# Attention in a decoder trunk: the two heads that share a 128-feature block are handled together, their matmuls side by side in halves of the array

## The chip, the cores and the metric

The kernel runs on one core of a Trainium2 chip. The metric is the device time of one execution in microseconds (us); the median of three runs before the change is 1267.95 us (1264.78 to 1268.28). The engines are named as the profile names them: PE (TensorE matmuls), PEld (its weight loads), DVE (VectorE), ACT (ScalarE), POOL (GpSimd) and SP (which here only issues DMAs).

## The reference

One inference step of a two-layer decoder trunk for a prompt of 512 tokens and 8 single-token samples (520 columns in all), model width 1024, all in float32. What matters here are two attentions; the rest (projections, retention in layer A, squared-ReLU MLPs of width 4096, norms) is untouched.

```
def memory_attention(q, mk, mv):                      # 4 heads of 64, 256 memory tokens, in both layers
    s = einsum('blhd,bmhd->bhlm', q, mk) * MEM_HD ** -0.5
    p = softmax(s, axis=-1)
    return einsum('bhlm,bmhd->blhd', p, mv)

def windowed_sink_attention(q, k, v, qpos, kpos, sinks):   # layer B: 12 heads of 64 over 4 kv heads
    dist = qpos[:, :, None] - kpos[:, None, :]
    valid = (kpos >= 0) & (dist >= 0) & (dist <= WINDOW)
    s = einsum('bnqgrd,bnkgd->bngrqk', q, k) * hd ** -0.5
    s = s - slopes * dist
    s = where(valid, s, -inf)
    p = sink_softmax(s, sink)                         # max over keys and the head's sink; the sink is in the sum
    return einsum('bngrqk,bnkgd->bnqgrd', p, v)
```

## The kernel before, in words

Activations lie feature-major: 128 features on the partitions, 520 tokens along the free axis. The big products (projections and MLP) use a split of every float32 operand into a high and a low part in a faster format (`product`, L233; three matmuls for each pair of tiles). The attentions use plain float32 matmuls; each of these appears in the trace as two PE records ("passes"), each with its own weight load.

Two heads of 64 features lie in one 128-feature block: head half `hh` = 0 on partitions 0 to 63, `hh` = 1 on partitions 64 to 127. A score matmul contracts over 64 features, so it uses 64 rows of the array (64\*128 in the trace); a value matmul ("PV" from here) gives 64 output features, so it uses 64 columns (128\*64).

**`mem_attention`** (L492 on; tiles `ms`, `p`, `mt`, `mpT`, `mo`) loops over the block `bl` (2) and the half `hh` (2). For each half it makes the scores of 4 blocks of 128 queries against 256 memory tokens, two blocks in one PSUM bank (L502), a softmax (row maximum on DVE L504, exp on ACT L506, scaling on DVE L511), transposes the probabilities on PE (L516), copies them out of PSUM (L518) and multiplies by the values, 512 columns at a time (L519). It runs in both layers.

**`win_pair`** (L653 on; tiles `ws`, `wp`, `wt`, `wpT`, `wo`) is called once for each of two blocks of kv heads `kb`, as the generators `w` and `W`, and loops over 4 query blocks `qb` and the halves `hh`. One half has three query heads: three score matmuls over 256 keys (128 in the first query block) into two PSUM banks of the role `ws` (L666), three additions of the distance penalty that read those banks (DVE L671), the sink softmax (L675 to L684 on DVE, exps on ACT L681), the scaling (L686, two of the three on POOL), three transposes for each key block (L692), a copy (ACT L694) and the PV matmul over 384 columns (L695). After both halves the output is split into its high and low part for the output projection (`Pair.put`, L177 on ACT and L178 on DVE).

PSUM has eight banks, given to roles: `mm` three (accumulators of the projections), `ws` two, `wt` two, `ot` one.

What sets the order: each phase is written as generators whose steps are woven by a string (`ORDER_A` for layer A with the memory attention as `a`; `ORDER_B` for layer B with `k` and `q` the projections, `a` the memory attention, `w`/`W` the two window generators, `s`/`S` the samples, `o` output projections). A step ends at `yield`. A scheduler then places the instructions of each engine, taking the string as the priority; where an instruction isn't ready it puts later matmuls ("filler": projection matmuls, L233) ahead of it.

Of the kernel before, what the change touches and what calls it, by code (L numbers as in the profile page):

```python
# [3 lines left out]

# [45 lines left out]
BUFS_A = dict(blk=2, qkv=6, wp=2, wpT=2, qw=1, kvs=1, ld=5)  # L50
BANKS = dict(mm=3, ws=2, wt=2, ot=1)
ORDER_A = "mhhhmhhhshkkhshkhshshkkkakhaakghhaghhhggghg"
ROLE_W = "ws"
BUFS_B = dict(blk=2, wp=4, wpT=6, ld=5)
# [5 lines left out]
ORDER_B = "kasakkskasqqsaqwqwqwqWWooSSSoSowWoWoo"  # L60
# [55 lines left out]
def build(tc, d, o):  # L116
    nc = tc.nc
    with ExitStack() as ctx:
# [372 lines left out]

        def mem_attention(l, qm, out):  # L492
            kT, v = memkv[l]
            for bl in range(2):
                for hh in range(2):
                    r = slice(64 * hh, 64 * hh + 64)
                    p = [blk(f"p{l}{bl}{hh}{qp}", [P, 2, MEM], "wp") for qp in range(2)]
                    for qp in range(2):
                        s = ps(f"ms{l}{bl}{hh}{qp}", "ws").rearrange("p (b m) -> p b m", b=2)
                        for b in range(2):  # L500
                            q0 = (2 * qp + b) * P
                            nc.tensor.matmul(s[:, b, :], qm[bl][r, q0:q0 + P], kT[r, bl, :], start=True, stop=True)  # L502
                        nm, sm, ri = (small(n, [P, 2]) for n in ("nm", "sm", "ri"))
                        nc.vector.tensor_reduce(out=nm, in_=s, axis=AX.X, op=ALU.max, negate=True)  # L504
                        for b in range(2):
                            nc.scalar.activation(out=p[qp][:, b, :], in_=s[:, b, :], func=AF.Exp,  # L506
                                                 bias=nm[:, b:b + 1], accum_out=sm[:, b:b + 1])
                        nc.vector.reciprocal(out=ri, in_=sm)
                        for b in range(2):
                            pb = p[qp][:, b, :]  # L510
                            nc.vector.tensor_scalar(out=pb, in0=pb, scalar1=ri[:, b:b + 1], scalar2=None, op0=ALU.mult)  # L511
                    pv = ps(f"mo{l}{bl}{hh}", "ot")
                    for mh in range(2):
                        t = ps(f"mt{l}{bl}{hh}{mh}", "wt")
                        for qb in range(NCH):
                            nc.tensor.transpose(t[:, qb * P:qb * P + P], p[qb // 2][:, qb % 2, mh * P:mh * P + P], ident)  # L516
                        pT = blk(f"mpT{l}{bl}{hh}{mh}", [P, T], "wpT")
                        (nc.scalar.copy if mh else nc.vector.tensor_copy)(out=pT, in_=t)  # L518
                        nc.tensor.matmul(pv[r, :], v[:, mh, (2 * bl + hh) * 64:(2 * bl + hh) * 64 + 64], pT,  # L519
                                         start=mh == 0, stop=mh == 1)  # L520
                    out.put(6 + bl, pv[r, :], slice(0, T), r)
                    yield
# [130 lines left out]
        def win_pair(kb, q, kT, vt, out, role):  # L653
            for qb in range(NCH):
                qs = slice(qb * P, qb * P + P)
                k0 = 0 if qb else P
                nk = 2 * P - k0
                ks = slice((qb - 1) * P + k0, qb * P + P)
                ot = ps(f"wo{kb}{qb}", "ot")
                for hh in range(2):  # L660
                    r = slice(64 * hh, 64 * hh + 64)
                    g = 2 * kb + hh
                    s = [ps(f"ws{g}{qb}{i}", role if i else "ws").rearrange("p (b m) -> p b m", b=2) for i in range(2)]
                    sv = [s[i // 2][:, i % 2, k0:] for i in range(3)]
                    for i in range(3):
# [410 lines left out]
```

## Time and profile before

| what | value |
|---|---|
| median of the three runs | 1267.95 us |
| the profiled execution's own time | 1268.36 us |
| its span, first to last instruction | 1266.0 us |
| PE busy | 1225.8 us (97%) |
| DVE busy | 861.7 us (68%) |
| ACT busy | 541.0 us (43%) |
| POOL busy | 309.5 us (24%) |
| mean granted TensorE clock | 0.979 of full speed |

The median and the profiled execution differ by 0.4 us, and the latter spends 2.4 us outside its span. A busy share is a mean over phases: layer A lies at about 0 to 288 us, its MLP follows, layer B with the window attention lies at about 688 to 863 us, and the second MLP ends the program. PE's busy time counts the tail of each matmul's pipeline, so for what a group of matmuls costs, the start of the next group in the timeline is the better reading.

### The profile page before, as it was taken

The page shows a single profiled execution, that of the slowest core. Times are in us where ns is not written, and L with a number is a line of the kernel's source. Part 1 is how long each engine was busy: PE and PEld are TensorE (multiplying, and loading weights), DVE is VectorE, ACT ScalarE, POOL GpSimd, SP SyncE. Part 2 cuts the span into 40 slices and gives each one's busy share as a digit, 9 for nine tenths or more (in the row PEclk, how much of TensorE's full clock was granted, in tenths as well). Part 3 has the DMA queues.
Part 4 walks back from the last instruction along what each step waited for, and adds up shares of the span by engine and source line. Part 5 has one row for each costly group of instructions (what it writes and reads, how often), then busy time and mean ns, then how long its engine had stood idle before and what let it go on. Part 6 is the DMA issues. An engine that isn't in the chain of part 4 may idle for free. (4 is left out here: it accounts for less than half of the span.)

```text
span 1266.0 us, 23737 instructions
## 1 busy us (share of the span) xinstructions
PE 1225.8 (97%) x9670; PEld 1152.8 (91%) x9670; DVE 861.7 (68%) x1615; ACT 541.0 (43%) x1019; POOL 309.5 (24%) x271
## 2 busy tenths in 40 slices
PE   8999999998899999999999999999799999999996
PEld 7999978898899999999999777577689999999996
DVE  7676766779886667666457556577996666676733
ACT  6232432234564444444324335445464444444532
POOL 2201100029321212121024112316731212131112
PEclk9999999998899999999999999899799999999998
DMA  8245512120232223232324341301123222222412
GB/s 303 103 152 181 196 58 82 69 101 34 84 113 88 101 85 117 84 117 84 117 84 141 132 147 45 123 1 35 34 101 111 90 101 100 92 95 98 143 41 69
DMA packets 43789, 128.26 MB, mean 101 GB/s; under 512 B 5112, under 2 KB 10368, under 8 KB 43552
## 3 DMA queue, kind: packets, MB, share of 16 engines
q1 hardware_dynamic: 41440, 119.80, 27.6%
q0 software_dynamic: 2240, 6.95, 1.5%
q8 instruction: 76, 1.25, 0.4%
q14 instruction: 33, 0.27, 0.1%
HBM read 117.65 MB, written 9.08 MB: 100 GB/s over the span
## 5 line engine op out<-in xcount | busy, mean ns | idle before, releaser
L433 DVE TENSOR_TENSOR xs<-d,xs 128x264 f32<-128x264 f32 (+1 forms) x128 | 53.9, 422 | 105.1 <-PE d L233 105.1
L785 ACT ACTIVATE u<-u 128x520 f32<-128x520 f32 x64 | 40.8, 637 | 29.6 <-DVE u L784 29.6
L233 PE MATMUL d<-hid,dw 128*128 128x256 f32 (+1 forms) x384 | 46.9, 283 | 0.0
L233 PEld LDWEIGHTS d<-hid,dw 128*128 128x128 f32 x384 | 46.3, 188 | 0.1
L619 POOL DMA_DIRECT2D out_ret_s<-s x12 | 6.8, 569 | 130.0 <-DVE S L599 64.7
L686 POOL TENSOR_SCALAR wp<-wp,wsm 128x256 f32<-128x256 f32 (+1 forms) x32 | 16.8, 535 | 68.8 <-DVE wsm L684 28.4
L784 DVE SCALAR_TENSOR_TENSOR u<-u,f0r 128x520 f32<-128x520 f32 x32 | 28.7, 898 | 0.4
L784 DVE SCALAR_TENSOR_TENSOR u<-u,f1r 128x520 f32<-128x520 f32 x32 | 28.6, 897 | 0.4
L681 ACT ACTIVATE wp<-wp,wnm 128x256 f32<-128x256 f32 (+1 forms) x48 | 22.7, 474 | 11.4 <-DVE wes L678 5.9
L233 PE MATMUL ob<-obh,obw 128*128 128x256 f32 (+1 forms) x128 | 26.0, 290 | 0.4 <-ACT obh L177 0.4
L178 DVE TENSOR_TENSOR hid<-u,hid 128x520 fp32r<-128x520 f32 x32 | 24.4, 761 | 0.0
L666 PE MATMUL ws<-kvb,qb 64*128 64x256 f32 (+1 forms) x96 | 23.9, 381 | 0.0
L233 PEld LDWEIGHTS ob<-obh,obw 128*128 128x128 f32 x128 | 20.4, 188 | 2.8 <-ACT obh L177 1.3
L671 DVE SCALAR_TENSOR_TENSOR wp<-cb,ws 128x256 f32<-128x256 f32 (+1 forms) x48 | 16.0, 380 | 6.8 <-PE ws L666 6.6
L177 ACT CAST hid<-u 128x520 fp32r<-128x520 f32 x32 | 20.1, 627 | 1.0
L253 POOL TENSOR_TENSOR f<-f0t,f 128x260 fp32r<-128x260 f32 x12 | 11.8, 982 | 33.6 <-ACT f L252 33.6
L666 PEld LDWEIGHTS ws<-kvb,qb 64*128 64x128 f32 x96 | 16.0, 192 | 4.3 <-issue 0.5
L695 PE MATMUL wo<-wpT,kvb 128*64 128x384 f32 x56 | 19.1, 530 | 0.7 <-ACT wpT L694 0.3
L694 ACT COPY wpT<-wt 128x384 f32<-128x384 f32 x28 | 12.6, 478 | 15.7 <-PE wt L692 15.5
L233 PE MATMUL ob<-obl,obw 128*128 128x256 f32 (+1 forms) x64 | 17.7, 292 | 0.3 <-DVE obl L178 0.3
L252 ACT CAST f<-f0t 128x260 fp32r<-128x260 f32 x16 | 6.5, 407 | 26.7 <-DVE f0t L263 26.7
L416 DVE SCALAR_TENSOR_TENSOR qb<-qb,br 128x256 f32<-128x256 f32 (+1 forms) x12 | 5.1, 425 | 18.2 <-PE qb L233 18.1
(2056 smaller groups left out, 5253.0 us busy)
## 6 DMA issues: line engine op xcount, KB each, us to landing
kc<-in_mem_k SPq DMA_DIRECT2D x16, 256.0 KB, 3.7
vc<-in_mem_v SPq DMA_DIRECT2D x16, 256.0 KB, 3.8
s<-in_S SPq DMA_DIRECT2D x12, 256.0 KB, 5.5
out_ret_s<-s POOLq DMA_DIRECT2D x12, 256.0 KB, 2.6
xs<-in_xT SPq DMA_DIRECT2D x8, 260.0 KB, 4.3
memx<-in_memT SPq DMA_DIRECT2D x1, 1024.0 KB, 8.6
u000r<-in_w_up SPq DMA_DIRECT2D x2, 512.0 KB, 3.1
u002r<-in_w_up SPq DMA_DIRECT2D x2, 512.0 KB, 3.9
```

The costliest lines, as they stand in the source:

```text
L177: nc.scalar.copy(out=self.hi(kt, sl, rows), in_=src)
L178: eng.tensor_sub(out=self.lo(kt, sl, rows), in0=src, in1=f(self.hi(kt, sl, rows)))
L233: nc.tensor.matmul(t, w[:, ws], a(kt, HALVES[s]), start=kt == k[0] and m == 0, stop=kt == k[-1] and m == 2)
L433: nc.vector.tensor_add(out=x[mb][:, ts], in0=t, in1=x[mb][:, ts])
L666: nc.tensor.matmul(sv[i], q[3 * kb + i][r, qs], kT[r, ks], start=True, stop=True)
L671: nc.vector.scalar_tensor_tensor(out=pv[:, i, :], in0=cb["nd"][:, k0:], scalar=float(SLOPES[hq + i]), in1=sv[i], op0=ALU.mult, op1=ALU.add)
L681: nc.scalar.activation(out=pv[:, i, :], in_=pv[:, i, :], func=AF.Exp, bias=nm[:, i:i + 1], accum_out=sm[:, i:i + 1])
L686: (nc.gpsimd if i in POOL_N else nc.vector).tensor_scalar(out=pv[:, i, :], in0=pv[:, i, :], scalar1=sm[:, i:i + 1], scalar2=1.0, op0=ALU.m ...
L694: nc.scalar.copy(out=pT, in_=t[:, 0:3 * P])
L695: nc.tensor.matmul(ot[r, 0:3 * P], vt[:, qb - 1 + kk, g * 64:g * 64 + 64], pT, start=kk == k0 // P, stop=kk == 1)
L784: nc.vector.scalar_tensor_tensor(out=u[i], in0=u[i], scalar=0.0, in1=r[0], op0=ALU.max, op1=ALU.mult)
L785: nc.scalar.square(out=u[i], in_=u[i])
```

## The change

`side_by_side` is new: it takes pairs of matmuls and adds an order-only dependency from each matmul to the one before it, so that the scheduler keeps the sequence half 1, half 0, half 1, half 0. `mem_attention` and `win_pair` handle both halves in one step: the scores of both (rows 0 to 63 and 64 to 127 of the array, into different PSUM banks), then, after a `yield`, the transposes of both and their PV matmuls (columns 0 to 63 and 64 to 127, into one bank). A window block's softmax now runs over six heads at once (`[P, 6]` statistics), its four score banks are two of `ws` and two of `mm` (`ROLE_W`), and the memory attention's output is split once for 128 partitions instead of twice for 64. Buffers change with it (`BUFS_A`, `BUFS_B`), and `ORDER_B` gives each window block two letters, one for the scores and one for the rest. In the changed file the lines move: scores and PV of both attentions are issued at L499, the transposes at L532 and L709, the window's additions at L686, its reduction at L690, its exps at L696 and its scaling at L701.

```
-BUFS_A = dict(blk=2, qkv=6, wp=2, wpT=2, qw=1, kvs=1, ld=5)
+BUFS_A = dict(blk=2, qkv=6, wp=2, mp=4, wpT=3, qw=1, kvs=1, ld=5)
-ROLE_W = "ws"
-BUFS_B = dict(blk=2, wp=4, wpT=6, ld=5)
+ROLE_W = "mm"
+BUFS_B = dict(blk=2, wp=3, mp=4, wpT=6, ld=5)
-ORDER_B = "kasakkskasqqsaqwqwqwqWWooSSSoSowWoWoo"
+ORDER_B = "kasakkskasqqsaqwqwqwwqWwWWwWooSSSoSowWWowoWWoo"
...
+        def side_by_side(*pairs):
+            last = None
+            for pair in pairs:
+                for m in reversed(pair):
+                    i = m()
+                    if last is not None:
+                        tc.add_manual_dep(i.ins, last.ins.name, mybir.DependencyInfo(
+                            mybir.DependencyClass.NoSync, mybir.DependencyReason.DATA), reason="side by side")
+                    last = i
...
             for bl in range(2):
-                for hh in range(2):
-                    r = slice(64 * hh, 64 * hh + 64)
-                    p = [blk(f"p{l}{bl}{hh}{qp}", [P, 2, MEM], "wp") for qp in range(2)]
-                    for qp in range(2):
-                        s = ps(f"ms{l}{bl}{hh}{qp}", "ws").rearrange("p (b m) -> p b m", b=2)
...
+                for qp in range(2):
+                    s = [ps(f"ms{l}{bl}{hh}{qp}", "ws").rearrange("p (b m) -> p b m", b=2) for hh in range(2)]
+                    side_by_side(*([partial(nc.tensor.matmul, s[hh][:, b, :], qm[bl][r, (2 * qp + b) * P:(2 * qp + b + 1) * P], kT[r, bl, :],
+                                            start=True, stop=True) for hh, r in enumerate(rows)] for b in range(2)))
...
+                yield
+                pv = ps(f"mo{l}{bl}", "ot")
+                for mh in range(2):
...
+                    side_by_side([partial(nc.tensor.matmul, pv[r, :], v[:, mh, (2 * bl + hh) * 64:(2 * bl + hh) * 64 + 64], pT[hh],
+                                          start=mh == 0, stop=mh == 1) for hh, r in enumerate(rows)])
-                    out.put(6 + bl, pv[r, :], slice(0, T), r)
+                out.put(6 + bl, pv, slice(0, T))
...
         def win_pair(kb, q, kT, vt, out, role):
...
+                s = [[ps(f"ws{kb}{qb}{hh}{i}", role if i else "ws").rearrange("p (b m) -> p b m", b=2) for i in range(2)]
+                     for hh in range(2)]
+                side_by_side(*([partial(nc.tensor.matmul, sv[hh][i], q[3 * kb + i][r, qs], kT[r, ks], start=True, stop=True)
+                                for hh, r in enumerate(rows)] for i in range(3)))
+                p = blk(f"wp{kb}{qb}", [P, 6, 2 * P], "wp")
...
+                m, nm, sm, es = (small(f"w{i}", [P, 6]) for i in ("m", "nm", "sm", "es"))
...
+                yield
...
+                    side_by_side([partial(nc.tensor.matmul, ot[r, 0:3 * P], vt[:, qb - 1 + kk, (2 * kb + hh) * 64:(2 * kb + hh) * 64 + 64],
+                                          pT[hh], start=kk == k0 // P, stop=kk == 1) for hh, r in enumerate(rows)])
```

How the instructions move, at three places. First PE near the end of layer B, before the change: the scores of one half (`ws320`: kv head 3, query block 2, bank 0), the PV matmuls of another (`wo03`: kb 0, query block 3; `wpT03` is kv head 0, the first half) and the first transpose (`wt13`) of the second half of that block.

```order
L666 MATMUL ws320_9741<-kvb_7825,qb0_7823 128x256
L666 MATMUL ws320_9741<-kvb_7825,qb1_7824 128x256
L666 MATMUL ws321_9742<-kvb_7825,qb1_7824 128x256
L695 MATMUL wo03_9613<-wpT030_9644,kvb_7825 64x384
L695 MATMUL wo03_9613<-wpT031_9651,kvb_7825 64x384
L692 MATMUL wt130_9680<-c_77,wp13_9659 128x128
```

The change, PE, in the middle of the window blocks: the six scores of block kb 1, qb 1 (the third digit of `ws1110` is the half), then the four PV matmuls of block kb 0, qb 1.

```order
L499 MATMUL ws1110_9129<-kvb_7819,qb0_7817 128x256
L499 MATMUL ws1100_9127<-kvb_7819,qb0_7817 128x256
L499 MATMUL ws1110_9129<-kvb_7819,qb1_7818 128x256
L499 MATMUL ws1100_9127<-kvb_7819,qb1_7818 128x256
L499 MATMUL ws1111_9130<-kvb_7819,qb1_7818 128x256
L499 MATMUL ws1101_9128<-kvb_7819,qb1_7818 128x256
L499 MATMUL wo01_8890<-wpT0110_8941,kvb_7819 64x384
L499 MATMUL wo01_8890<-wpT0100_8935,kvb_7819 64x384
L499 MATMUL wo01_8890<-wpT0111_8955,kvb_7819 64x384
L499 MATMUL wo01_8890<-wpT0101_8949,kvb_7819 64x384
```

The halves, which stood in separate groups, now alternate.

Second, PE in the memory attention of layer A after the change (`ms`: layer, block, half, query pair; `rt` is a transpose of the retention, `ga` a gate projection).

```order
L499 MATMUL ms0111_2122<-memk0_1089,orq1_97 128x256
L595 MATMUL rt40_2398<-c_77,k4_2000 128x128 x3
L499 MATMUL ms0101_2121<-memk0_1089,orq1_97 128x256
L499 MATMUL ms0111_2122<-memk0_1089,orq1_97 128x256
L499 MATMUL ms0101_2121<-memk0_1089,orq1_97 128x256
L595 MATMUL rt40_2398<-c_77,k4_2000 128x128
L234 MATMUL ga101_2589<-ah1_189,ga1h_2558 128x264
L499 MATMUL mo00_2060<-mpT0011_2089,memv0_1090 64x512
L499 MATMUL mo00_2060<-mpT0001_2082,memv0_1090 64x512
```

Here the first matmul of the sequence stands alone, ahead of other work, and three follow together; the two PV matmuls stand together.

Third, PE at the end of layer B's window blocks after the change: the end of block kb 0, qb 3, then matmuls of the samples (`wst`, `wso`, `wsx`), then the scores of kb 1, qb 2.

```order
L499 MATMUL ws0311_9545<-kvb_7819,qb0_7817 128x256
L499 MATMUL ws0301_9543<-kvb_7819,qb0_7817 128x256
L756 MATMUL wst1_9461<-c_77,wsp1_9416 128x128
L757 MATMUL wst1_9461<-c_77,wsp1_9416 8x128
L763 MATMUL wso1_9468<-wvn_9312,wpn_9466 128x256
L770 MATMUL wso1_9468<-vwc4_9470,wspT1_9464 32x256 x2
L770 MATMUL wso1_9468<-vwc6_9475,wspT1_9464 32x256 x2
L776 MATMUL wsx1_9482<-c_77,wsosb1_9480 128x128 x2
L499 MATMUL ws1210_9585<-kvb_7819,qb0_7817 128x256
```

Before the change these sample matmuls stood among output-projection matmuls; here none stands between them.

## Rows read from the trace of the kernel before

**Rows 1.** The page, busy time, share and instructions of each engine (first line).

```profile
PE 1225.8 (97%) x9670; PEld 1152.8 (91%) x9670; DVE 861.7 (68%) x1615; ACT 541.0 (43%) x1019; POOL 309.5 (24%) x271
```

**Rows 2.** Windows of the attention stretches: us, busy PE, PEld, DVE, ACT, POOL, granted clock, DMA.

```profile
150.00:230.00 80.00, 80.00 (x572) 66.92 (x571) 53.15 (x146) 27.32 (x61) 4.84 (x8) 1.00 0.22 78
690.00:748.00 58.00, 58.00 (x397) 44.33 (x397) 31.91 (x81) 19.72 (x54) 9.81 (x7) 1.00 0.37 117
748.00:785.30 37.30, 37.30 (x228) 28.54 (x227) 24.05 (x85) 17.61 (x61) 10.44 (x17) 1.00 0.20 61
785.30:815.40 30.10, 28.06 (x157) 17.46 (x156) 19.60 (x66) 17.07 (x55) 12.85 (x15) 0.83 0.52 173
815.40:863.00 47.60, 46.43 (x297) 35.08 (x297) 29.19 (x123) 21.40 (x84) 7.51 (x15) 1.00 0.00 1
```

**Rows 3.** Groups by line (forms apart or mixed): count, busy us, mean ns, idle before.

```profile
L666 PE MATMUL ws<-kvb,qb 64*128 64x256 f32 (+1 forms) x96 | 23.9, 381 | 0.0
L502 PE MATMUL ms<-memk,orq 64*128 64x256 f32 x32 | 9.5, 408 | 0.0
L502 PE MATMUL ms<-memk,qb 64*128 64x256 f32 x32 | 8.2, 392 | 0.0
L519 PE MATMUL mo<-mpT,memv 128*64 128x512 f32 x32 | 16.1, 610 | 0.0
L695 PE MATMUL wo<-wpT,kvb 128*64 128x384 f32 x56 | 19.1, 530 | 0.7 <-ACT wpT L694 0.3 <-DVE obl L178 0.3
L233 PE MATMUL d<-hid,dw 128*128 128x256 f32 (+1 forms) x384 | 46.9, 283 | 0.0
```

**Rows 4.** Timeline of PE around two score groups: start us, us, operation, count.

```profile
172.23 1.13 PE L502 MATMUL ms<-memk,orq 64*128 64x256 f32 x4
173.29 0.39 PE L233 MATMUL qkv<-ah,qkv42l 128*128 128x256 f32 x1
...
759.41 0.28 PE L233 MATMUL qb<-bh,qb4h 128*128 128x256 f32 x1
759.62 1.56 PE L666 MATMUL ws<-kvb,qb 64*128 64x256 f32 x6
761.11 0.38 PE L233 MATMUL qb<-bl,qb4h 128*128 128x256 f32 x1
```

**Rows 5.** Timeline of PE around three PV groups of the window attention.

```profile
766.53 0.86 PE L695 MATMUL wo<-wpT,kvb 128*64 128x384 f32 x2
767.32 0.39 PE L233 MATMUL qb<-bh,qb4l 128*128 128x264 f32 x1
...
852.99 1.50 PE L695 MATMUL wo<-wpT,kvb 128*64 128x384 f32 x4
854.42 0.39 PE L233 MATMUL ob<-obl,obw 128*128 128x264 f32 x1
...
794.71 1.52 PE L695 MATMUL wo<-wpT,kvb 128*64 128x384 f32 x8
796.16 0.39 PE L233 MATMUL ob<-obl,obw 128*128 128x256 f32 x1
```

**Rows 6.** Timeline of PE at the longest idle gap of the window attention.

```profile
800.60 0.68 PE L723 MATMUL wss<-kwc,qdw 128*32 128x129 f32 x8 [1.64 <-DVE wp L671]
```

**Rows 7.** Groups by line with forms apart: the window softmax between scores and transposes.

```profile
L671 DVE SCALAR_TENSOR_TENSOR wp<-cb,ws 128x256 f32<-128x256 f32 x36 | 13.2, 413 | 5.9 <-PE ws L666 5.8
L675 DVE TENSOR_REDUCE wm<-wp 128x3 f32<-128x768 f32 x12 | 11.4, 948 | 0.1
L681 ACT ACTIVATE wp<-wp,wnm 128x256 f32<-128x256 f32 x36 | 18.0, 500 | 8.9 <-DVE wes L678 4.7 <-DVE wnm L677 4.0
L681 ACT ACTIVATION_READ_ACCUMULATOR wp<-wp,wnm 128x1 f32 x48 | 9.1, 189 | 0.0
L686 POOL TENSOR_SCALAR wp<-wp,wsm 128x256 f32<-128x256 f32 x24 | 12.8, 545 | 54.0 <-DVE wm L676 28.1 <-DVE wsm L684 20.1 <-DVE wes L678 3.7
L694 ACT COPY wpT<-wt 128x384 f32<-128x384 f32 x28 | 12.6, 478 | 15.7 <-PE wt L692 15.5
```

More of the change, by code (lines that the diff above doesn't have):

```diff
@@ L3 @@
 from contextlib import ExitStack, contextmanager
+from functools import partial
 import numpy as np
@@ L494, in mem_attention @@
             for bl in range(2):
-                for hh in range(2):
-                    r = slice(64 * hh, 64 * hh + 64)
-                    p = [blk(f"p{l}{bl}{hh}{qp}", [P, 2, MEM], "wp") for qp in range(2)]
-                    for qp in range(2):
-                        s = ps(f"ms{l}{bl}{hh}{qp}", "ws").rearrange("p (b m) -> p b m", b=2)
-                        for b in range(2):
[L501 to L506, printed above, removed]
+                p = {}
@@ L653, in win_pair @@
         def win_pair(kb, q, kT, vt, out, role):
+            rows = [slice(0, 64), slice(64, P)]
             for qb in range(NCH):
@@ L656, in win_pair @@
                 k0 = 0 if qb else P
[L657 removed]
                 ks = slice((qb - 1) * P + k0, qb * P + P)
+                kbs = range(k0 // P, 2)
                 ot = ps(f"wo{kb}{qb}", "ot")
[L660 to L665, printed above, removed]
[L666 to L696 removed]
@@ new lines, in win_pair @@
+                pv = p[:, :, k0:]
+                for j in range(6):
+                    nc.vector.scalar_tensor_tensor(out=pv[:, j, :], in0=cb["nd"][:, k0:], scalar=float(SLOPES[6 * kb + j]),
+                                                   in1=sv[j // 3][j % 3], op0=ALU.mult, op1=ALU.add)
+                m, nm, sm, es = (small(f"w{i}", [P, 6]) for i in ("m", "nm", "sm", "es"))
+                sk = sinks[:, 6 * kb:6 * kb + 6]
+                nc.vector.tensor_reduce(out=m, in_=pv, axis=AX.X, op=ALU.max)
@@ new lines, in win_pair @@
+                nc.vector.tensor_max(out=m, in0=m, in1=sk)
+                nc.vector.tensor_scalar(out=nm, in0=m, scalar1=-1.0, scalar2=None, op0=ALU.mult)
+                nc.vector.tensor_sub(out=es, in0=sk, in1=m)
+                nc.scalar.activation(out=es, in_=es, func=AF.Exp)
+                for j in range(6):
+                    nc.scalar.activation(out=pv[:, j, :], in_=pv[:, j, :], func=AF.Exp, bias=nm[:, j:j + 1],
+                                         accum_out=sm[:, j:j + 1])
@@ new lines, in win_pair @@
+                nc.vector.tensor_add(out=sm, in0=sm, in1=es)
+                nc.vector.reciprocal(out=sm, in_=sm)
+                for j in range(6):
+                    (nc.gpsimd if j % 3 in POOL_N else nc.vector).tensor_scalar(
+                        out=pv[:, j, :], in0=pv[:, j, :], scalar1=sm[:, j:j + 1], scalar2=1.0, op0=ALU.mult, op1=ALU.mult)
+                yield
+                for kk in kbs:
+                    pT = []
+                    for hh in range(2):
+                        t = ps(f"wt{kb}{qb}{hh}{kk}", "wt")
+                        for i in range(3):
+                            nc.tensor.transpose(t[:, i * P:i * P + P], p[:, 3 * hh + i, kk * P:kk * P + P], ident)
+                        pT.append(blk(f"wpT{kb}{qb}{hh}{kk}", [P, 3 * P], "wpT"))
+                        nc.scalar.copy(out=pT[hh], in_=t[:, 0:3 * P])
+                    side_by_side([partial(nc.tensor.matmul, ot[r, 0:3 * P], vt[:, qb - 1 + kk, (2 * kb + hh) * 64:(2 * kb + hh) * 64 + 64],
+                                          pT[hh], start=kk == k0 // P, stop=kk == 1) for hh, r in enumerate(rows)])
```

55 lines of the change are left out of this document (14 added, 41 removed).

## The prediction

> **What bounds the kernel now.** I read the busy shares first: PE is busy for 97% of the span [rows 1]. The share is a mean, so the attention stretches come next, cut into windows [rows 2]: in layer A's (150 to 230 us) and in layer B's up to 785.3 us PE is busy without a gap at the full clock, while DVE has 55 to 66% and ACT a third to a half. [...] So PE sets the pace nearly everywhere, and what counts is what PE spends on the attention matmuls. The groups by line give their counts [rows 3]; what one costs I read from the timeline.
>
> **Price of a pass.** A group of four score passes of 256 columns starts at 172.23 us and the next work at 173.29: 1.06 us. A group of six takes 759.62 to 761.11: 1.49 us [rows 4]. Two more passes cost 0.43, so one costs 0.215, and 0.20 is left as a fixed cost. Ahead of the group the last projection matmul needs 0.21 us (759.41 to 759.62) where a stream of them needs 46.9 / 384 = 0.122 [rows 3, 4]: another 0.09. So each excursion into 64-row matmuls costs 0.29 beside its passes. For PV, two passes of 384 columns take 0.79 and four 1.43 us [rows 5]: 0.32 each, 0.15 fixed, with the same 0.09 ahead 0.24 for an excursion. A memory PV pass has 512 columns: 0.32 x 512 / 384 = 0.427, an estimate.
>
> **Do halves run abreast?** For PV the old trace shows it. At 794.71 us eight passes stand together and take 1.45 us [rows 5]: the order has both matmuls of the first half, then both of the second (block kb 0, qb 2). One after the other they would need 8 x 0.32 + 0.15 = 2.71; four passes need 1.43. So the column halves ran wholly abreast, though not interleaved in the order. [...] For the score halves (64 rows) no row shows two abreast. The bounds are no gain and a full halving; below nothing I exclude, since two halves that take turns cost what they cost now. I take the halving, because the nearest row, the PV group of eight on the same engine, shows one.
>
> **The sum on PE, before.** Scores: the window's 96 passes are 72 of 256 columns (15.5 us) and 24 of 128 (2.6 at half the price), the memory's 64 make 13.8: 31.9. PV: 32 x 0.427 = 13.7 and 56 x 0.32 = 17.9, less 2.6 because two groups of eight already run abreast: 29.0. The order of PE has 33 score and 27 PV excursions: 33 x 0.29 + 27 x 0.24 = 16.1. Together 77.0; the busy times of the five groups add up to 76.8 [rows 3], so the prices hold.
>
> **After.** PV is two heads in the time of one: 16 x 0.427 + 28 x 0.32 = 15.8, a gain of 13.2. The scores would halve to 16.0, but the order often lets the first matmul of a sequence stand alone (second place in the section on the change): four times in layer A, three in layer B's memory attention, and in two window blocks. Counted in slots: memory 24 + 22 and window 40 of 256 columns, 12 of 128: 86 x 0.215 + 12 x 0.108 = 19.8, a gain of 12.1. Excursions fall to 27 and 17: 11.9, a gain of 4.2. PE saves 29.5 us in all: about 11 in the memory attentions, 18.5 in the window attention.
>
> **What else moves.** Statistics over six heads at once save DVE 68 instructions and ACT 23 in the order; both engines wait for PE in these stretches [rows 2], so I price that at nothing, and it costs nothing if that cover goes. The transposes and their copies keep their number. The scaling on POOL stays behind the same stores in POOL's queue, and SP's loads keep their order but for a few in layers A and B; POOL is busy for under half of any stretch [rows 2].
>
> **New waits.** A window block's softmax chain, from scores to the first transpose, doubles: six additions x 0.413 = 2.5, a reduction twice as wide 1.9, six exps with their read-outs 6 x 0.69 = 4.1, two scalings on POOL 1.1 [rows 7], and some 1 us of small operations: 10.6 us. And a block now holds four banks (two `ws`, two `mm`) until its additions have read them, so the next block's scores wait for these. Three places have little filler:
> - Scores of kb 1 qb 0 and kb 0 qb 2 stand one behind the other: the second waits for six half-wide additions (1.2 to 2.5 us), half of it beside the first's own passes: 1 us. Then kb 1 qb 1 waits for six full ones, 2.5 us, of which twelve transposes cover over half: 1 us.
> - At the third place of the section on the change the samples' matmuls wait for copies of about half a microsecond (a comparable copy takes 0.478 [rows 7]) three times with nothing between: 2 us.
> - At the end, between the last scores and their transposes, PE has 39 projection matmuls (4.8 us), two PV pairs (1.8) and 24 transposes of earlier blocks (about 3): 9.6 against 10.6, so 1 us.
>
> That is 5 us; the ends are 0 (the filler is enough) and 12 (another microsecond at each of the remaining hand-offs). The present gap of 1.64 us [rows 6] may go, but the same stretch gets shorter cover, so I leave it and the lower clock where they are.
>
> **Sum.** 1268.4 (the profiled execution, 2.4 us outside its span) - 29.5 + 5 = **1244 us**. The median of the runs, 1267.95, stands 0.4 below that execution, less than I can resolve.
>
> **Rivals.**
> - Better: no new wait, and the gap of 1.64 us and most of the stretch at the lower clock go, worth up to 4 us: 1268.4 - 29.5 - 5.6 = 1233 us. For it: DVE and ACT have room [rows 2]. Against: the softmax chain is longer than the filler at three places. Chance 0.13.
> - The change does not do all it says: the score halves take turns, as no row shows otherwise. Then only PV (13.2) and excursions (4.2) are won: 1268.4 - 17.4 + 5 = 1256. Or halves overlap only where the order interleaves them, the last pass of each group being alone: a lone PV pair then takes three slots for two, a group of n alternating matmuls n + 1; that costs 12 lone PV pairs (4.7), five PV groups of four (1.6) and about 1.8 in the scores, 8.1 in all: 1252. [...] The group of eight speaks against it. Chance together 0.13.
> - The gain is eaten exactly, within 0.3% (3.8 us, about what a measurement of this kernel can tell from no change): waits of 26 to 33 us. Chance 0.07.
> - Slower: the four banks. Where output-projection accumulators hold the `mm` banks, no window block can start its scores, the six blocks after 785 us run one after the other, and PE stands through most of each chain. At 7 of the 10.6 us for six blocks that is 42 us: 1268.4 - 29.5 + 42 = 1281. It decides from 33 / 6 = 5.5 us a block. For it: the lower clock and the gap of today lie in this very stretch [rows 2, 6]. Against: the new order puts the scores of three blocks ahead of the accumulators, and up to 785 us PE has filler. [...] Chance 0.06.
>
> **How the numbers follow.** The forecast has 0.61. The range goes from the better case, 1233, to 1260, which takes in both figures of the second rival, and the forecast with 12 us of waits (1251) or some 16 more than I count. Left out are the two cases without gain and a little more: under 0.2. Faster 0.87 (the forecast, the better case and the second rival), within 0.3% 0.07, slower 0.06.
>
> **What would show it.** In the changed profile a window block's twelve score passes of 256 columns should take about 6 x 0.215 + 0.2 = 1.5 us in the timeline (2.8 if the halves take turns); a lone pair of PV matmuls, four passes of 384 columns, 0.8 us (1.1 if the order holds them), four PV matmuls 1.45; the memory's PV pair 1.0. Layer A's attention should end 5 to 6 us earlier relative to its start, layer B's about 19 with the waits. PE idle in the windows after 785 us should name DVE or ACT for some 5 us. I am wrong if PE shows over 10 us of idle there, if the granted clock falls for longer than the present 10 us, or if the score groups keep their length.

## The result and the profile after

The changed kernel takes 1252.16 us (median of 4 runs, 1249.86 to 1253.98) where the kernel before took 1267.24 in the same comparison: a ratio of 0.9883 (95% interval 0.986 to 0.9905), 15.1 us. The forecast was 1244, the range 1233 to 1260. The profiled execution took 1251.94 us. From the page of the changed kernel, its span and its first line of busy times [rows 1]:

```profile
span 1250.2 us, 23651 instructions
...
PE 1200.6 (96%) x9670; PEld 1140.9 (91%) x9670; DVE 853.5 (68%) x1563; ACT 537.6 (43%) x1007; POOL 310.0 (25%) x271
```

PE lost 25.2 us of busy time (1225.8 to 1200.6) and the span only 15.8. So PE got cheaper by most of the 29.5 us that were forecast, and part of it came back as idle time. First the prices: PE's timeline of the changed kernel around paired groups (start us, us with the pipeline's tail, operation, passes) [rows 4, 5]:

```profile
683.48 1.13 PE L499 MATMUL ms<-memk,qb 64*128 64x256 f32 x8
684.54 0.39 PE L234 MATMUL kv<-bh,kv1l 128*128 128x264 f32 x1
...
703.83 1.08 PE L499 MATMUL mo<-mpT,memv 128*64 128x512 f32 x4
704.84 0.66 PE L532 MATMUL mt<-c,p 128*128 128x128 f32 x4
...
757.30 0.87 PE L499 MATMUL wo<-wpT,kvb 128*64 128x384 f32 x4
758.10 0.39 PE L234 MATMUL qb<-bh,qb5l 128*128 128x264 f32 x1
...
769.92 1.51 PE L499 MATMUL wo<-wpT,kvb 128*64 128x384 f32 x8 [0.57 <-DVE obl L179]
771.36 0.39 PE L234 MATMUL ob<-obh,obw 128*128 128x256 f32 x1
...
805.66 1.56 PE L499 MATMUL ws<-kvb,qb 64*128 64x256 f32 x10
807.15 0.33 PE L756 MATMUL wst<-c,wsp 128*128 128x128 f32 x1
```

Eight score passes take 1.06 us, what four took before. Ten, a window block's twelve without its first matmul, which stood alone earlier, take 1.49, what six took: the half that still has all three of its matmuls, six passes, sets the length. The memory's PV pair takes 1.01, a lone window pair 0.80, two pairs 1.44. Every one of these is the price that the prediction gave.

Now the account of layer B's attention. I cut it at the first matmul of its first q projection (`qb6`) and at the last PV matmul, and again at the last q projection. Windows (from:to, us, busy us and count of PE, PEld, DVE, ACT, POOL, granted clock, DMA share, GB/s), first the kernel before:

```profile
662.30:785.40 123.10, 122.52 (x848) 99.77 (x847) 76.83 (x201) 48.95 (x134) 31.27 (x32) 1.00 0.33 109
785.40:860.90 75.50, 72.67 (x442) 51.20 (x440) 48.20 (x186) 37.58 (x135) 18.80 (x27) 0.93 0.21 69
```

The changed kernel:

```profile
654.20:760.70 106.50, 105.08 (x810) 89.75 (x809) 64.72 (x160) 38.22 (x105) 25.22 (x23) 1.00 0.39 125
760.70:844.40 83.70, 71.07 (x474) 51.32 (x472) 54.53 (x177) 45.73 (x156) 23.66 (x35) 0.92 0.19 64
```

Layer B begins 8.1 us earlier (662.3 to 654.2; layer A's attention gives 7.4 of that). Up to the last q projection another 16.6 us are won (123.1 to 106.5), and behind it 8.2 are given back (75.5 to 83.7): PE does less there (72.67 to 71.07, although more of the window blocks lies behind that point) and stands idle for 12.6 us where it stood for 2.8. Who waits, from the waits of the changed kernel (engine, line and tile that waited, what ended it: us in total, times, longest), 654 to 846 us:

```profile
PE wt L709 <- POOL wp L701: 3.5, 7, 1.9
PE wt L709 <- ACT wpT L711: 1.4, 5, 0.6
PE wso L763 <- DVE wpn L761: 1.2, 1, 1.2
PE ob L234 <- ACT obh L178: 1.2, 3, 0.6
PE wss L740 <- DMA kwc<-in_swa_k: 0.8, 1, 0.8
PE ws L499 <- DVE wp L686: 0.6, 1, 0.6
PE wsx L776 <- ACT wsosb L773: 0.5, 1, 0.5
```

Before the transposes (`wt`) PE waits for the scaled probabilities, the last step of the softmax. But no wait is long; the rest is spread over eight more pairs of 1.0 us or less. Windows of the same kernel behind the last q projection:

```profile
761.00:781.00 20.00, 14.91 (x120) 10.04 (x119) 19.85 (x46) 12.28 (x31) 12.02 (x10) 1.00 0.59 193
781.00:798.00 17.00, 13.69 (x72) 8.15 (x73) 7.33 (x31) 12.68 (x48) 5.85 (x13) 0.90 0.22 83
798.00:815.00 17.00, 15.29 (x102) 11.20 (x103) 11.45 (x52) 4.44 (x20) 0.00 (x0) 0.85 0.01 1
815.00:830.00 15.00, 12.94 (x84) 11.72 (x83) 12.52 (x40) 7.17 (x28) 3.86 (x8) 0.84 0.01 1
```

DVE has 19.85 of the first 20 us. Its costliest groups there (count, busy us, mean ns, idle before):

```profile
L686 DVE SCALAR_TENSOR_TENSOR wp<-cb,ws 128x256 f32<-128x256 f32 x12 | 4.3, 406 | 0.0
L690 DVE TENSOR_REDUCE wm<-wp 128x6 f32<-128x1536 f32 x2 | 3.5, 1740 | 0.0
L736 DVE COPY kwc<-kvb 128x2 f32<-128x2 f32 x2 | 1.9, 990 | 0.0
L216 DVE TENSOR_TENSOR obw<-ob2r,obw 128x1024 fp32r<-128x1024 f32 x1 | 1.8, 1781 | 0.0
```

Three blocks' softmax (kb 1 qb 0, kb 0 qb 2, kb 1 qb 1) and the splitting of the output-projection weights (four subtractions L216, 5.4 us together) meet in this stretch. In the kernel before, kb 0 qb 2 had been scored beside the q projections.

### The profile page after: what moved, and what is told of

Same layout as the page of the kernel before. It is cut to its first block, busy times and chain, and to the rows that moved or that the text cites. A ratio compares the mean times of both kernels' runs of the same rounds, so it can differ in the third digit from the quotient of the medians.

```text
span 1250.2 us, 23651 instructions
## 1 busy us (share of the span) xinstructions
PE 1200.6 (96%) x9670; PEld 1140.9 (91%) x9670; DVE 853.5 (68%) x1563; ACT 537.6 (43%) x1007; POOL 310.0 (25%) x271
## 5 line engine op out<-in xcount | busy, mean ns | idle before, releaser
L801 DVE SCALAR_TENSOR_TENSOR u<-u,f0r 128x520 f32<-128x520 f32 x32 | 29.7, 932 | 0.4
L701 POOL TENSOR_SCALAR wp<-wp,wsm 128x256 f32<-128x256 f32 (+1 forms) x32 | 15.5, 496 | 55.7 <-ACT wp L696 25.7
L696 ACT ACTIVATE wp<-wp,wnm 128x256 f32<-128x256 f32 (+1 forms) x48 | 22.5, 470 | 11.3 <-DVE wes L693 7.4
L520 ACT ACTIVATE p<-ms,nm 128x256 f32<-128x256 f32 x32 | 14.8, 475 | 18.5 <-DVE nm L518 16.8
L709 PEld LDWEIGHTS wt<-c,wp 128*128 128x128 f32 x84 | 9.9, 148 | 12.6 <-POOL wp L701 6.6
L709 PE MATMUL wt<-c,wp 128*128 128x128 f32 x84 | 16.1, 302 | 5.1 <-POOL wp L701 3.5
L254 POOL TENSOR_TENSOR f<-f0t,f 128x260 fp32r<-128x260 f32 x12 | 11.8, 982 | 27.8 <-ACT f L253 27.8
L518 DVE TENSOR_REDUCE nm<-ms 128x2 f32<-128x512 f32 x16 | 10.3, 685 | 11.8 <-PE ms L499 11.8
L179 DVE TENSOR_TENSOR obl<-wo,obh 128x128 fp32r<-128x128 f32 x24 | 6.9, 287 | 15.1 <-ACT obh L178 15.0
L499 PE MATMUL ws<-kvb,qb 64*128 64x256 f32 (+1 forms) x96 | 15.6, 407 | 1.1 <-DVE wp L686 0.6
```

The source lines that it names most:

```text
L179: eng.tensor_sub(out=self.lo(kt, sl, rows), in0=src, in1=f(self.hi(kt, sl, rows)))
L254: eng.tensor_sub(out=l, in0=src, in1=f(h))
L499: i = m()
L520: nc.scalar.activation(out=t[:, b, :], in_=s[hh][:, b, :], func=AF.Exp, bias=nm[:, b:b + 1], accum_out=sm[:, b:b + 1])
L696: nc.scalar.activation(out=pv[:, j, :], in_=pv[:, j, :], func=AF.Exp, bias=nm[:, j:j + 1], accum_out=sm[:, j:j + 1])
L701: (nc.gpsimd if j % 3 in POOL_N else nc.vector).tensor_scalar(out=pv[:, j, :], in0=pv[:, j, :], scalar1=sm[:, j:j + 1], scalar2=1.0, op0=A ...
```

## The experiments

All times are medians; each comparison had its own runs of the kernel before (1267.24 to 1267.97), so the differences to it are what I compare.

**Which part yields.** mem_only and win_only each take over one of the two attentions from the change.

```
mem_only: win_pair, ORDER_B, ROLE_W of the kernel before; mem_attention of the change
win_only: mem_attention of the kernel before; win_pair, ORDER_B, ROLE_W of the change
```

> Only the two memory attentions are paired; the window attention and layer B's order are those of the kernel before. My theory: the memory part yields nearly what PE saves there by the prices (11 us), since projections fill its softmax waits: 11 to 13 us under the kernel before, 1254 to 1257 us, and the last q projection ends some 12 us earlier with no new wait behind it. Rival: the pairing costs waits wherever it is used; then the memory part gives 6 us or less, 1261 us or more.

> Only the window attention is paired; the memory attentions are those of the kernel before. My theory: the window part is where the missing gain is lost. The matmuls get cheaper by 18.5 us on PE, but three softmax chains stand without filler behind the last q projection, so only 3 to 5 us are left: 1262 to 1265 us. Rival: the parts add up as the prediction's sum had it and something common to both is lost; then this one is 13 us faster than the kernel before, 1254 us.

Measured: mem_only 1253.67 (0.9897, 0.988 to 0.9913), 14.3 under the kernel before; win_only 1264.38 (0.9978, 0.9969 to 0.9988), 3.6 under it. Nearly the whole gain of the change is the memory attention's; on top of it the window part adds 0.8 us (15.1 - 14.3), which the intervals can't tell from nothing. win_only is where its theory had it; mem_only gained a little more than its theory's 11 to 13 us. mem_only in the same windows:

```profile
655.10:769.20 114.10, 112.52 (x836) 95.19 (x834) 74.21 (x196) 44.19 (x121) 28.38 (x29) 1.00 0.37 117
769.20:845.60 76.40, 70.60 (x455) 50.40 (x453) 48.68 (x190) 40.40 (x146) 23.23 (x29) 1.00 0.22 70
```

This lets the window part be taken apart. What PE would spend at the full clock I estimate as its busy time less span x (1 - granted clock), the loss in stretches at the lower level. (In the change an output-projection matmul starts 0.21 us after the one before it from 814.84 to 816.12 us, where the granted clock is 0.50, and 0.12 us after it from 816.80 to 817.86, where it is 1.00.) All in us, from the windows above (the last two kernels come below):

| first q to last PV | span | PE busy | clock loss | PE at full clock | PE idle |
|---|---|---|---|---|---|
| before | 198.6 | 195.2 | 5.3 | 189.9 | 3.4 |
| changed | 190.2 | 176.2 | 6.7 | 169.5 | 14.0 |
| mem_only | 190.5 | 183.1 | 0 | 183.1 | 7.4 |
| thin_single | 182.7 | 179.8 | 0 | 179.8 | 2.9 |
| thin_paired | 176.2 | 170.4 | 1.4 | 169.0 | 5.8 |

From mem_only to the change PE saves 13.6 us. 6.6 come back as idle time and 6.7 as lower clock; 0.3 us of the span is left. (The clock is read to 0.01, which is 0.8 us in such a window.) mem_only itself did bring new waits behind the last q projection, against its theory (idle there 5.8 us where it was 2.8); what lifted its gain is that the 5.3 us of lower clock are gone.

Two limits of this table. Each row is one profiled execution; over mem_only's four executions the mean granted clock of the whole program was 0.980 to 0.986, so how a loss splits into idle time and clock may vary. And mem_only and thin_single issue the same matmuls here, yet stand at 183.1 and 179.8: the column "PE at full clock" holds some 3 us that are not the matmuls' own price.

**Does the order of the halves matter?**

```
 def side_by_side(*pairs):
-    for pair in pairs:
-        for m in reversed(pair):
+    for half in reversed(list(zip(*pairs))):
+        for m in half:
```

> The matmuls of a pair group stand half by half in the program (all scores of the second head, then all of the first) where the change has them in turns. My theory: halves run abreast whatever the order, as the old PV group of eight did; a window group of twelve 256-column passes still takes 1.5 us, a memory group of eight 1.06, and the time is that of the change, 1250 to 1255 us. Rival: matmuls start and end in program order, so only the last of one half and the first of the other overlap; then the group of twelve takes some 10 x 0.215 + 0.2 = 2.35 us and the group of eight 1.5, 13 us more in all: about 1265 us.

Measured: 1253.90 (0.9892, 0.9877 to 0.9907), 14.1 under the kernel before. PE's timeline of no_turns:

```profile
685.80 1.14 PE L499 MATMUL ms<-memk,qb 64*128 64x256 f32 x8
686.87 0.39 PE L234 MATMUL kv<-bh,kv1l 128*128 128x264 f32 x1
...
753.87 2.10 PE L499 MATMUL ws<-kvb,qb 64*128 64x256 f32 x12
755.90 0.87 PE L499 MATMUL wo<-wpT,kvb 128*64 128x384 f32 x4
...
825.38 2.10 PE L499 MATMUL ws<-kvb,qb 64*128 64x256 f32 x12
827.41 0.38 PE L234 MATMUL ob<-obh,ob6h 128*128 128x256 f32 x1
```

The group of eight, four passes of one half and then four of the other, still takes 1.07 us: wholly abreast, as my theory had it. For the twelve neither figure is right: both groups of 256 columns at the full clock take 2.03 us, (2.03 - 0.20) / 0.215 = 8.5 slots, where turns give six and one half after the other twelve. So the second half does start while the first runs, but not before some of it is done: it reached over four passes, not over six. The rival is not borne out either: with a slot of 0.215 us and 0.20 fixed it would give the group of eight six slots, 1.49 us, and the group of twelve ten, 2.35, if each matmul's two passes count as one (seven and eleven slots, 1.71 and 2.57 us, if passes count singly), and the rows are shorter. In other blocks the order put a half by itself (765.67 to 767.16 us and 767.94 to 769.43, 1.49 us each for six passes). That is where this kernel's score time went; in sum it lost 1 us against the change, within the intervals.

**Single waits behind the last q projection.** Four kernels each move one suspect out of the dense stretch.

```
 hold:      c = nc.scalar.copy(out=wh, in_=raw)          # chunk.fill
+           if name in ("ob4", "ob5", "ob6"):
+               tc.add_manual_dep(c.ins, last_exp[1, 1].ins.name, NoSync)
 early:    -t = half(f"obw{mb}", ...) if mb < KEEP else None
           +t = half(f"obw{mb}", ...) if mb >= 3 else None
 pool_subs: -POOL_W = (1, 4, 5)
            +POOL_W = (0, 1, 2, 3, 4, 5, 6)
 order1:   -ORDER_B = "kasakkskasqqsaqwqwqwwqWwWWwWooSSSoSowWWowoWWoo"
           +ORDER_B = "kasakkskasqqsaqwqwqwwwqWwWWWooSSSoSowWWowoWWoo"
```

> The change, but on ACT the casts of the three output-projection weights that wait for their loads (ob4, ob5, ob6) stand behind the last exp of the third window block after the last q projection, not ahead of the first block's exps. My theory: these casts hold up ACT's queue (idle 4.8 us on loads, 3.1 us of casts) while the first block's exps stand ready; with them out of the way those exps start at about 771 us where they now start at 777.35, PE's idle time between 761 and 798 falls by 3 to 6 us, and the kernel takes 1246 to 1249 us. Rival: the chains are held by DVE and POOL as much, or the late casts are missed later by the output projection; then the time stays within 1.5 us of the change's, 1251 to 1254 us.

hold measured 1255.28 (0.9907, 0.989 to 0.9924), 12.7 under the kernel before: slower than the change by 2.4, worse than either theory had it, though the intervals overlap. (The profiled execution, 1258.44, is the slowest of its four.) ACT's timeline at the first exp of the first block, of hold and then of the change:

```profile
775.91 0.40 ACT L700 ACTIVATE wp<-wp,wnm 128x128 f32<-128x128 f32 x1 [2.22 <-DVE wes L697]
```

```profile
777.35 0.40 ACT L696 ACTIVATE wp<-wp,wnm 128x128 f32<-128x128 f32 x1
```

That is 14.1 us behind its last q matmul (761.78), where the change has 16.6 (777.35 - 760.75): the casts did stand in the way, for 2.5 us, and behind them the exps wait for DVE. The casts then ran later, and PE's timeline of hold shows the bill, beside DVE's and POOL's:

```profile
796.84 2.83 PE L503 MATMUL wo<-wpT,kvb 128*64 128x384 f32 x8 [3.98 <-DVE obl L180]
```

```profile
790.03 3.09 DVE L220 TENSOR_TENSOR ob6l<-ob6r,ob6h 128x1024 fp32r<-128x1024 f32 x1 [1.55 <-ACT ob6h L216]
793.05 2.29 DVE L755 TENSOR_TENSOR wssm<-wssm,wses 128x1 f32<-128x1 f32 x1
```

```profile
792.00 3.32 POOL L220 TENSOR_TENSOR ob5l<-ob5r,ob5h 128x1024 fp32r<-128x1024 f32 x1
```

A subtraction for a weight that is needed much later stands in DVE's queue ahead of the low part of an output that PE needs at once. But its place in the queue is only part of the bill. In the change the same subtraction takes 1.21 us and the one-column operation behind it 0.14; here they take 3.09 and 2.29, and the second ends when POOL's subtraction does, at 795.3 us, which itself takes 3.32 us for 2.40. So where DVE and POOL's subtractions met, both ran longer. In the change too: the two copies of two columns (L736, 1.9 us together) run beside POOL's subtraction of ob5 (775.22 to 777.62 us); in hold, without it, they take 0.23. ACT's queue was not the bound; DVE was suspected next.

> The change, but of the seven output-projection weights that are split ahead of time, the first three (ob0 to ob2) go into the buffers that the q weights leave, and the last four into the halves that come free after the last q projection (it was the other way round), so that two casts on ACT and one or two subtractions (1.2 us each on DVE) can run beside the q projections. My theory after the first four runs: DVE bounds the stretch after the last q projection, 19.85 of 20 us busy between 761 and 781; every microsecond taken from it there brings the first window block's transposes forward by as much. This moves one DVE subtraction out and the late casts' waits with it: 1.5 to 3 us faster than the change, 1249 to 1251 us. Rival: ACT and POOL or the clock hold it, and nothing changes: 1252 to 1254 us.

> The change, but all seven subtractions that split these output-projection weights run on POOL, where three did: DVE loses four of them (1.21 + 1.78 + 1.21 + 1.21 = 5.4 us) between 761 and 781, POOL gets four of 2.4 us, 9.6 us more. My theory (DVE bounds that stretch): the first block's transposes start some 4 us earlier, and 2 to 5 us of it reach the end, 1248 to 1251 us. Rival: the scaling of the probabilities on POOL then waits behind the subtractions (POOL had 17.9 us of work between 761 and 798 and gets 27.5), and the time is the change's or up to 3 us more, 1253 to 1256 us.

> The change with one step of layer B's order moved: the scores of kb 0 qb 2 stand ahead of the last q projection instead of behind it and its PV step two places earlier, so that one of the three softmax chains (on DVE six additions of 0.345 us, a reduction of 1.74, small operations: 4.5 us; six exps on ACT) runs beside projections, as in the kernel before. My theory (DVE bounds the stretch after the last q projection): 3 to 6 us faster than the change, 1247 to 1250 us, and DVE has idle time between the last q projection and the first output. Rival: the last q projection is held up by the score banks (a block now holds two of the three mm banks) and what is won behind is lost ahead: within 1.5 us of the change.

early measured 1253.50 (0.9896, 0.9879 to 0.9912), 14.0 under the kernel before. From the last q projection to the last output projection it took 104.0 us where the change takes 107.2, as the theory said; from there to the last matmul 378.4 where the change takes 373.8, so that in all it is at the rival's figure. pool_subs measured 1254.18 (0.9899, 0.9884 to 0.9913), 13.3 under. Its windows show that DVE was relieved (15.55 of the first 20 us) and that PE got no busier for it:

```profile
761.00:781.00 20.00, 14.26 (x93) 9.86 (x94) 15.55 (x40) 13.62 (x44) 13.17 (x13) 0.83 0.24 79
781.00:798.00 17.00, 12.69 (x83) 7.89 (x83) 10.84 (x27) 9.43 (x31) 12.47 (x14) 0.96 0.69 217
```

It isn't a clean test, though, for POOL's added subtractions met DVE's operations. DVE's timeline of pool_subs in the first block's chain, beside POOL's subtraction of ob2 (769.71 to 772.05 us):

```profile
770.23 1.86 DVE L692 TENSOR_SCALAR wnm<-wm 128x6 f32<-128x6 f32 x1
```

The next of this kind, at 774.04 us, takes 0.17. order1 measured 1251.92 (0.9879, 0.9865 to 0.9894), 15.6 under: its last q matmul comes 2.1 us later (the scores stand ahead of it), the stretch behind is 1.5 us shorter, and its PE is no less idle (15.8 us from the first q projection to the last PV, 14.0 in the change). So no run shows DVE's load alone to be the bound either. Then the length of one chain, and the spreading of chains:

```
 per_head:   -m, nm, sm, es = (small(..., [P, 6]) ...)   # one set for six heads
             +for hh in range(2): m, nm, sm, es = (small(..., [P, 3]) ...)
 head_order: per_head, and
             -ORDER_B = "...qWwWWwWooSSSoSowWWowoWWoo"
             +ORDER_B = "...qWwWWwwWWooSSSoSowWoWoWoo"
 head_early: per_head and early, and
             -for mb in range(KEEP + 3): project_out(mb, 1)
             +for mb in (3, 4, 5, 6, 0, 1, 2): project_out(mb, 1)
```

> The change with paired matmuls, but the window softmax's statistics, exps and scalings for each head by itself, as in the kernel before: the chain to a head's first transpose is half as long, while DVE gets the 68 small instructions back (0.15 to 0.9 us each). A rival of the DVE theory: it is the length of the chain (10.6 us in the prediction) that PE waits for; then this is 3 to 6 us faster than the change, 1247 to 1250 us. My theory (DVE's work bounds it, not the chain's length): no gain, 1252 to 1256 us.

> per_head with another order behind the last q projection: the scores of the fourth block of kb 0 and the third of kb 1 stand ahead of the output projections, so that two more softmax chains run while the output projections fill PE (ACT has 12 of 17 us idle between 798 and 815 in the change). If the softmax work is what bounds, spreading it into that stretch gives 2 to 6 us against per_head: 1245 to 1249 us. Rival: the added chains only delay the first blocks, whose outputs the output projections wait for; then it is 1251 us or more.

> per_head and early together, and the second pass of the output projections in another order (the four weights in halves first, the three in the weight buffers last), so that the halves come free for the MLP as they did in the change. early shortened the stretch from the last q projection to the last output projection by 3.2 us (107.2 to 104.0) and per_head by 2.1 (to 105.1), but behind it early took 378.4 us to the end where the change takes 373.8. If those 4.6 us came from the halves being held longer, this one keeps 373.8 behind and wins 2 to 4 us against the change in front of it: 1247 to 1250 us, under both kernels. Rival: the 4.6 us have another cause (the weight buffers, the loads' order), and it stays at 1252 or more.

per_head measured 1251.10 (0.9873, 0.9859 to 0.9888), 16.4 under the kernel before, and head_order 1251.11 (0.987, 0.9852 to 0.9887), 16.6 under. Against the change's 15.1 that is 1.3 and 1.5 us, and the intervals overlap: no version is shown to be faster than the change, and head_order is at its rival's figure. head_early measured 1262.93 (0.9966, 0.9954 to 0.9978), only 4.6 under. In front it won nothing (107.1 us from the last q to the last output projection, so the gains of its two parts do not add), and behind it took 383.6 us where the change takes 373.8. From 866 to 930 us its PE waits 11.3 us for `f`, which the MLP reads (7.9 for DVE, 3.4 for ACT), where the change's waits 1.0 (its longest wait there, 5.1, is for `xs`; head_early's for that is 2.5). One window of it at the entry of the MLP, and then of the change:

```profile
880.00:895.00 15.00, 7.52 (x27) 6.15 (x28) 12.67 (x17) 6.59 (x17) 13.19 (x13) 0.50 0.10 35
```

```profile
880.00:895.00 15.00, 12.58 (x55) 11.52 (x55) 13.42 (x20) 5.26 (x13) 10.16 (x9) 0.50 0.17 50
```

The MLP's first operands come later. That halves were held longer, as I had put it for early, is not borne out, since here they came free first; which buffer or queue it is was not settled.

**The softmax as a whole.** If no single piece gives the time back, all of it together should.

```
 thin_paired: the change;  thin_single: mem_only;  in win_pair of both
-  reduce, max, negate, sub, exp of the sinks, exps per head, add, reciprocal, scalings
+  nc.scalar.activation(out=pv, in_=pv, func=AF.Exp)
```

> The change with most of the window softmax left out: after the six additions one exp over the whole block, no maximum, no sums, no scaling (so the probabilities are not normalised). To be read beside the next kernel, which has the same cut with window heads one by one. My theory now: what eats the window part's gain is not one wait but the softmax work of DVE, ACT and POOL as a whole, which a block needs longer for than PE does for the paired matmuls; hold, early and pool_subs moved single pieces of it and each changed little. With that work gone, the pairing of the window matmuls must be worth most of the 18.5 us that PE saves: this kernel 10 to 17 us faster than the next. Rival: the gain is lost to PSUM banks, the order of the program or the clock, which are the same here; then it is 5 us or less.

> Memory attentions paired, window heads one by one as in the kernel before, and the same cut of the window softmax (one exp for each head's block, no maximum, sums or scaling). My theory: PE sets the pace here already in the kernel with the full softmax, so the cut is worth little, 2 to 8 us under 1253.7, and the paired kernel beside it is 10 to 17 us faster still. Rival: it gains as much from the cut as the paired one, and the two stay within 5 us.

Measured: thin_single 1245.30 (0.9824, 0.981 to 0.9839), 22.4 under the kernel before; thin_paired 1238.02 (0.9767, 0.9753 to 0.9782), 29.7 under. Windows of thin_single:

```profile
654.60:771.20 116.60, 115.02 (x852) 96.57 (x850) 66.56 (x157) 42.75 (x97) 24.70 (x20) 1.00 0.36 114
771.20:837.30 66.10, 64.78 (x437) 48.08 (x437) 30.68 (x116) 29.45 (x75) 8.92 (x7) 1.00 0.26 80
```

and of thin_paired:

```profile
654.60:761.80 107.20, 105.43 (x816) 90.53 (x815) 62.47 (x151) 37.73 (x86) 24.18 (x19) 1.00 0.39 124
761.80:830.80 69.00, 64.94 (x473) 47.13 (x472) 34.07 (x123) 32.12 (x78) 9.83 (x7) 0.98 0.24 77
```

With the softmax cut, pairing the window heads is worth 7.3 us, with the whole softmax 0.8. Neither theory had that: I expected 10 to 17, the rival at most 5. The table takes it apart: PE saves 10.8 us (179.8 to 169.0), of which 2.9 come back as idle time and 1.4 as clock, where the full softmax took 6.6 and 6.7 of 13.6. So the softmax work is what turns most of the window part's gain into idle time and lower clock: 13.3 us come back with it, 4.3 without (one execution each; by the medians 0.8 and 7.3 us are left). The heads one by one were held by it too, more than I had expected: thin_single is 8.1 us better than mem_only, thin_paired 14.6 better than the change. The cut frees three engines and shortens each chain at once; which of these counts most, the pair doesn't tell. What is left has other causes: the PE saving is smaller than forecast, and thin_paired still waits at the samples' hand-offs (1.2 us at `wso`, 0.5 at `wsx`, as in the change).

## Why the prediction was right, and where it was not

- **The prices on PE** held to 0.05 us for each kind of group. The score halves ran abreast (eight passes in 1.06 us, what four took before), the bound that I took between no gain and a full halving. The counts of small instructions were off, without bearing on the sum: DVE lost 52 and ACT 12 (1615 to 1563, 1019 to 1007), not 68 and 23.
- **The sum on PE**: forecast 29.5. Measured: 20.4 in layer B (189.9 to 169.5) and 7.4 in layer A's attention (the first MLP starts at 294.72 us where it started at 302.08), 27.8 together. The split was off: the memory attentions gave some 14 (7.4, and 6.8 in layer B from before to mem_only) where I had 11, the windows 13.6 where I had 18.5. (With the softmax cut the windows' saving reads 10.8, so that column is known to some 3 us.)
- **New waits: this is the term that was mis-sized.** I had 5 us with 12 as the upper end. Measured in layer B: 14.0 of idle time for 3.4, which is 10.6, and 1.4 us more of lower clock, 12.0 together. 27.8 - 10.6 - 1.4 = 15.8 us, what the profiled spans differ by (1266.0 - 1250.2; the MLPs' own differences, under 1 us each, cancel). The hand-offs that I priced came out near their price: 0.6 us before the scores of kb 0 qb 2, none before those of kb 1 qb 1, 1.2 and 0.5 at the samples (`wso`, `wsx`), 1.9 behind the last scores, 4.2 together. What I left out is the rest, most of it between 762 and 798 us: there three blocks' softmax met the splitting of seven weights within 20 us, DVE was busy for 19.85 of them (16.91 in the 20 us behind the last q projection before), and what waited was the next in every queue: fifteen kinds of wait in layer B, the longest 1.9 us. Costing one chain at a time could not show that; the sum of the other engines' work per window behind the last q projection could have pointed at it, though the runs do not show DVE's share alone to decide.
- **The chain itself** was priced too long, not too short: an exp with its read-out follows the next after 0.49 us in both kernels, as the two overlap, not after 0.69, so six take 2.9 us and not 4.1.
- **"It costs nothing if that cover goes"** for the statistics of six heads at once was right about itself: undoing it (per_head) changed less than the intervals tell.
- **The clock**: I left it where it was. In layer B's attention the loss is nearly the same (5.3 and 6.7), but it is not the same stretch, and mem_only's profiled execution shows what could have been had: no loss at all. The change has 13.7 us at the lower level there (782.4 to 785.8 and 809.7 to 816.6 us at a granted clock of 0.51, 826.8 to 830.2 at 0.50), the kernel before 10.2 (800.5 to 810.7 at 0.50), which are the "present 10 us" of the prediction: the second of my signs of being wrong.
- **"Layer B about 19 us earlier with the waits"** was 8.4 (198.6 to 190.2), and the idle time behind the last q projection, 12.6 us, passed the 10 us that I had named as the sign of being wrong. The largest kind of wait ended with POOL's scaling (3.5 us), where I had named DVE or ACT. The range held because its upper part allowed for 12 us of waits, and because layer A gave 7.4 us where I had 5 to 6. That the change gained about what was forecast is luck in part: the windows, from which I had most of the saving, yielded 0.8 us, and mem_only's 14.3 us are about the whole gain.
- **The rivals**: the four PSUM banks did not decide (1.7 us of waits at `ws` and `ob` end with additions, L686 and L743). Turn-taking did not happen; that the time is 1252 us, the second figure of that rival, is a coincidence: no run shows the last pass of each group alone, on which that figure rests, since the paired groups took no longer than full overlap (1.06 us for eight score passes, 0.80 for a lone PV pair). The slow case had the right place, the six blocks behind the last q projection, and a price far too high: the idle time there grew by 9.8 us (2.8 to 12.6), 1.6 for each block, not 7.

## What to carry to other kernels

When a change makes the busiest engine's part of a block cheaper, add up what the other engines do for that block and compare over the stretch in which the blocks stand together, not chain by chain: here the gain held where projections filled PE (the memory attentions) and nearly vanished where little but blocks was left. Test the parts of such a change apart; one of the two here was worth nearly nothing. When moving a single piece out of the way doesn't help, cut all of that kind of work at once: that told the softmax from the remaining causes in two runs.

## What the runs showed of the hardware

Matmuls in different halves of the array ran abreast here without alternating in the program: a group of four plus four passes, half by half, took 1.07 us for rows, where four took 1.06, and in the kernel before 1.45 us for columns, where four took 1.43 [rows 4, 5]. Six plus six were not wholly abreast (2.03 us, twice, where turns take 1.49 by the price of a pass). How far the second half reaches ahead was seen at these two lengths only.

Operations of DVE that met a subtraction on POOL ran longer, down to one column (2.29 us for 0.14 in hold, and 1.86 for 0.17 in pool_subs); no run was made to separate the two.

Behind the last q projection of the change the lower clock came after stretches in which PE stood and started, and fell on the work that followed. Windows of the change around the first two lower stretches there:

```profile
776.00:782.40 6.40, 4.02 (x32) 3.17 (x32) 6.11 (x16) 5.25 (x22) 4.70 (x7) 1.00 0.88 284
782.40:785.80 3.40, 3.15 (x15) 2.74 (x14) 0.37 (x3) 3.40 (x16) 0.42 (x2) 0.51 0.80 317
...
803.00:809.70 6.70, 5.47 (x45) 4.18 (x44) 5.26 (x31) 2.01 (x10) 0.00 (x0) 1.00 0.00 1
809.70:816.60 6.90, 6.42 (x33) 4.50 (x26) 5.87 (x26) 1.53 (x7) 0.00 (x0) 0.51 0.00 0
```

PE was busy for 4.02 of 6.4 us and for 5.47 of 6.7, and then ran at a granted clock of 0.51 for 3.4 and 6.9 us. mem_only had a window just as thin without a fall behind it (its clock is 1.00 to the last PV):

```profile
790.00:796.00 6.00, 3.32 (x22) 1.96 (x21) 2.38 (x11) 2.56 (x10) 2.97 (x6) 1.00 0.82 308
```

So 2.4 us of idle time before the first fall were followed by a loss of 1.7 us through the clock (3.4 x 0.49), 1.2 us before the second by 3.4 (6.9 x 0.49), and 2.7 us in mem_only by none; what decides was not tried.
